# Output products of a four-layer hybrid trunk: plain products against Strassen's seven block products

## The chip, the cores and the metric

The kernel runs on one core of a Trainium2 chip. The metric is the device time of one execution in microseconds; the median of three runs stands for a kernel. The trace is that of one profiled execution. Five engines matter: TensorE (PE, matmuls and transposes), VectorE (DVE), ScalarE (ACT), GpSimd (POOL) and SyncE (SP), whose queue starts the DMAs. Each engine runs its own queue strictly in order, and engines wait for each other on semaphores.

## The reference

A decoder trunk of four layers on x of 1024 tokens by 1024 features, float32. Each layer normalizes, mixes tokens and adds an output product:

```python
for layer in range(DEPTH):                  # 4
    xn = rms_norm(x, norm_w[layer])
    kind, idx = layer % N_MIXERS, layer // N_MIXERS   # fox, gla, gdn, fox
    ...
    x = x + y.astype(x.dtype)
# each mixer ends with
    return (o * jax.nn.silu(z)) @ w_out     # o, z: 1024 x 1024; w_out: 1024 x 1024
```

FoX is softmax attention over 8 heads with a forget gate, GLA a gated linear attention over 4 heads, GDN (Gated DeltaNet) a chunked delta rule over 8 value heads. The change concerns the last line, `(o silu(z)) @ w_out`, and the addition to x.

## The kernel before, in words

Every float32 product is made of rounded parts: a value is split into `hi` (rounded, on ACT, L118) and `lo` (the rest, a subtraction on DVE, L119; `Trunk.split`), and `Trunk.mm3` issues three matmuls, hi by hi (L123), hi by lo (L124) and lo by hi (L125). The array `act` holds the transposed left side of the product at hand in both parts, eight token tiles of 128 by eight K tiles of 128 features.

A layer runs in this order. `Normed.scale` and `Normed.turn` scale a token tile by its norm (L63) and transpose it on PE (L207, into PSUM banks `pt`); L118 and L119 split it into `act`. The mixer projects its heads from `act`, computes them, gates them, and puts o into `oT` (FoX, already transposed: L411 on POOL multiplies by the gate) or `oN`/`og`/`o` (GLA, GDN), from where it goes into `act` again. Then `Trunk.out_proj` (L212) walks over chunks of output columns, 384, 384 and 256 wide in FoX, four of 256 in GLA and GDN (`MixPool.OUT`). `wchunk` loads and splits the chunk's weights. For each token tile a PSUM bank `pj` collects 8 K tiles by 3 matmuls, DVE adds it to x in place (L225), and ACT takes the sum of squares of the new x (L230). With the last chunk each finished token tile is stored, its norm taken (`rsqrt`, L130 on POOL), scaled and transposed for the next layer, tile by tile while later tiles are still in the product.

In FoX, the attention of a query tile t runs logits (`pq`), row maximum on DVE (L362), exponential on ACT (L369, `Lg`), scaling on DVE (L373), transposes on PE (L383, L387), a split (`PT<-pt`, L118 and L119), and the product with V (`pv<-PT,V`), which ACT copies to `oT` (L398).

The order of each engine's queue is not written by hand: the kernel is built in a context that schedules by a simulated timeline, within the program's dependences and the buffers of `MixPool` (tags with a number of buffers each; a new tile waits for the release of the old one). Weight chunks of the output product have buffers of their own among the weights, so its first matmuls can be placed between the last ones of the mixer.

## Time and profile before

| | us |
|---|---|
| median of 3 runs | 2326.18 |
| lowest, highest | 2325.18, 2328.27 |
| span of the profiled execution | 2328.1 |
| PE busy | 2256.5 (97%) |
| DVE busy | 1284.5 (55%) |
| ACT busy | 1026.5 (44%) |
| POOL busy | 424.5 (18%) |

The profiled execution's own time is its span of 2328.1 us, from the first to the last instruction; it is close to the slowest of the three runs. Busy time is the sum of an engine's instructions; matmuls overlap each other in the pipe, so one lasts longer in a row than the distance to the next. The granted clock of PE is given as a share of full speed. The trace puts the output products (first to last L225) at 556.9 to 649.8, 1012.5 to 1106.6, 1595.3 to 1712.7 and 2235.6 to 2325.1 us.

### The profile page before, as it was taken

The page shows a single profiled execution, that of the slowest core. Times are in us where ns is not written, and L with a number is a line of the kernel's source. Part 1 is how long each engine was busy: PE and PEld are TensorE (multiplying, and loading weights), DVE is VectorE, ACT ScalarE, POOL GpSimd, SP SyncE. Part 2 cuts the span into 40 slices and gives each one's busy share as a digit, 9 for nine tenths or more (in the row PEclk, how much of TensorE's full clock was granted, in tenths as well). Part 3 has the DMA queues.
Part 4 walks back from the last instruction along what each step waited for, and adds up shares of the span by engine and source line. Part 5 has one row for each costly group of instructions (what it writes and reads, how often), then busy time and mean ns, then how long its engine had stood idle before and what let it go on. Part 6 is the DMA issues. An engine that isn't in the chain of part 4 may idle for free.

```text
span 2328.1 us, 41807 instructions
## 1 busy us (share of the span) xinstructions
PE 2256.5 (97%) x15694; PEld 2143.1 (92%) x15694; DVE 1284.5 (55%) x3564; ACT 1026.5 (44%) x3046; POOL 424.5 (18%) x680
## 2 busy tenths in 40 slices
...
DMA packets 177626, 140.93 MB, mean 61 GB/s; under 512 B 37232, under 2 KB 165104, under 8 KB 177424
## 3 DMA queue, kind: packets, MB, share of 16 engines
...
q8 instruction: 123, 2.02, 0.4%
q14 instruction: 79, 0.65, 0.1%
...
## 4 chain that ended last, share of the span: by engine, by line
PE 79%; DMA 8%; POOL 4%; DVE 3%; issue 2%; ACT 2%; SPq 1%; ACTq 0%; POOLq 0%; DVEq 0%
PE pj L123 20%; PE pj L125 20%; PE pj L124 19%; DMA raw<-in_fox_w_in_dram 4%; POOL xt L800 2%; POOL tm L798 2%; PE pv L124 2%; PE pv L125 2%; PE pt L207 1%; PE pt L387 1%; PE pv L123 1%; PE pq L123 1%; PE pq L125 1%; PE pq L124 1%; PE pt L383 1%
## 5 line engine op out<-in xcount | busy, mean ns | idle before, releaser
L123 PE MATMUL pj<-w,act 128*128 128x256 f32 (+3 forms) x2688 | 855.8, 319 | 20.5 <-DVE x L225 5.8
L125 PE MATMUL pj<-w,act 128*128 128x256 f32 (+3 forms) x2688 | 844.7, 314 | 0.0
L124 PE MATMUL pj<-w,act 128*128 128x256 f32 (+3 forms) x2688 | 843.3, 314 | 0.4 <-DVE w L163 0.2
L123 PEld LDWEIGHTS pj<-w,act 128*128 128x128 f32 x2688 | 512.9, 191 | 35.0 <-ACT w L162 8.5
L124 PEld LDWEIGHTS pj<-w,act 128*128 128x128 f32 x2688 | 513.1, 191 | 3.9 <-DVE w L163 1.4
L125 PEld LDWEIGHTS pj<-w,act 128*128 128x128 f32 x2688 | 511.8, 190 | 3.1 <-DVE act L119 0.6
L163 DVE SCALAR_TENSOR_TENSOR w<-raw,nw,w 128x256 fp32r<-128x256 f32 (+4 forms) x443 | 217.7, 511 | 164.0 <-ACT w L162 162.4
L162 ACT ACTIVATE w<-raw,nw 128x256 fp32r<-128x256 f32 (+4 forms) x443 | 212.1, 506 | 216.4 <-DMA raw<-in_fox_w_in_dram 146.9
L123 PE MATMUL pj<-act,w 128*128 128x256 f32 (+1 forms) x896 | 305.0, 340 | 1.4 <-ACT y L686 1.4
L125 PE MATMUL pj<-act,w 128*128 128x256 f32 (+1 forms) x896 | 303.6, 339 | 2.4 <-DVE w L163 2.2
L124 PE MATMUL pj<-act,w 128*128 128x256 f32 (+1 forms) x896 | 303.3, 339 | 0.0
L130 POOL TENSOR_TENSOR rs<-ss,mhalf 128x2 f32<-128x2 f32 (+2 forms) x152 | 112.0, 737 | 634.4 <-DVE ss L129 553.5
L125 PEld LDWEIGHTS pj<-act,w 128*128 128x128 f32 x896 | 172.9, 193 | 20.0 <-DVE w L163 3.5
L123 PEld LDWEIGHTS pj<-act,w 128*128 128x128 f32 x896 | 173.0, 193 | 17.7 <-ACT y L686 2.0
L124 PEld LDWEIGHTS pj<-act,w 128*128 128x128 f32 x896 | 172.8, 193 | 15.5
L225 DVE TENSOR_TENSOR x<-x,pj 128x256 f32<-128x256 f32 (+1 forms) x112 | 51.1, 457 | 156.4 <-PE pj L125 152.8
L369 ACT ACTIVATE Lg<-Lg,nm 128x128 f32<-128x128 f32 (+7 forms) x128 | 99.3, 776 | 60.4 <-DVE nm L368 53.6
L294 ACT ACTIVATE qk<-pj 128x128 f32<-128x128 f32 x256 | 68.5, 273 | 113.5 <-PE pj L125 80.9
L119 DVE TENSOR_TENSOR PT<-pt,PT 128x512 fp32r<-128x512 f32 (+1 forms) x160 | 97.5, 631 | 29.2 <-ACT PT L118 28.8
L118 ACT CAST PT<-pt 128x512 fp32r<-128x512 f32 (+1 forms) x160 | 80.8, 543 | 68.7 <-PE pt L387 68.7
L411 POOL TENSOR_TENSOR oT<-oT,g 128x256 f32<-128x256 f32 x64 | 46.4, 743 | 274.1 <-DVE g L408 234.8
L688 DVE SCALAR_TENSOR_TENSOR y<-u,cw,y 128x512 f32<-128x512 f32 x96 | 77.9, 814 | 26.4 <-ACT y L686 23.2
...
## 6 DMA issues: line engine op xcount, KB each, us to landing
raw<-in_fox_w_in_dram SPq DMA_DIRECT2D x123, 192.0 KB, 3.6
...
raw<-in_fox_w_in_dram SPq DMA_DIRECT2D x128, 64.0 KB, 2.1
...
```

The lines of the kernel that those rows point to most:

```text
L118: self.nc.scalar.copy(hi, src)
L119: self.nc.vector.tensor_tensor(lo, src, hi.bitcast(F32), ALU.subtract)
L123: mm(out, lhi, rhi, start=start, stop=False)
L124: mm(out, lhi, rlo, start=False, stop=False)
L125: mm(out, llo, rhi, start=False, stop=stop)
L130: self.nc.gpsimd.tensor_tensor(out, ss, self.mhalf[:, :n], ALU.pow)
L162: self.nc.scalar.activation(hi, r, AF.Copy, scale=f)
L163: self.nc.vector.scalar_tensor_tensor(lo, r, f, hi.bitcast(F32), ALU.mult, ALU.subtract)
L225: nc.vector.tensor_tensor(xr, xr, p, ALU.add)
L294: nc.scalar.activation(qk[:, i, :], p[:, i * DH:(i + 1) * DH], AF.Square, accum_out=ss[:, i:i + 1])
L369: nc.scalar.activation(L[:, :W], L[:, :W], AF.Exp, bias=nm[:, 0:1], accum_out=nm[:, 1:2])
L688: stt(y, u[:, j:j + 512], cw[:, j, blk:blk + 1], y, ALU.mult, ALU.add)
```

## The change

The output product A W (A = o silu(z)) is done on halves: A11, A12, A21, A22 are halves of tokens by halves of features, B11 to B22 halves of features by halves of output columns. Winograd's form of Strassen's scheme needs seven block products instead of eight, with S1 = A21 + A22, S2 = S1 - A11, S3 = A11 - A21, S4 = A12 - S2 on the left, and differences of the B blocks on the right (made in place in the raw buffers on POOL: L367, L369, L374, L380). Each product is 4 token tiles by 4 K tiles by 3 matmuls of 256 columns, and the whole is run twice (`i` = 0, 1), for 256 columns of each column half. Results are added to x on DVE straight from PSUM or on POOL from the intermediate U.

This is the loop that goes, in `out_proj`, and the end of `fox`:

```diff
-        for i, n in enumerate(mp.out_widths):
-            w = self.wchunk([(0, self.cols(w_out, c0, n=n))], n)
-            for t in range(NT):
-                xr = x[t][:, c0:c0 + n]
-                p = self.pj()[:, :n]
-                self.proj_tok(p, t, w, 0, n)
-                nc.vector.tensor_tensor(xr, xr, p, ALU.add)
-                if nxt is None:
-                    nc.sync.dma_start(dst[t][:, c0:c0 + n], xr)
-                    continue
-                sq = mp.tile([P, D], mybir.dt.bfloat16, tag=mp.roles["sq"], name="sq")
-                nc.scalar.activation(sq[:, :n], xr, AF.Square, accum_out=parts[:, t, i:i + 1])
-                if i + 1 == nch:
-                    nc.sync.dma_start(dst[t], x[t])
-                    ss = total[:, t:t + 1]
-                    nc.vector.tensor_reduce(ss, parts[:, t, :], mybir.AxisListType.X, ALU.add)
-                    nxt.scale(t, ss)
-                    nxt.turn(t - 2)
-            c0 += n
         gate(H - 2)
         gate(H - 1)
-        for t in range(NT):
-            self.split(self.act[:, t, 0], self.act[:, t, 1], oT[t // 2][:, :, t % 2 * P:t % 2 * P + P])
...
+        mp.to_tail()
+        return self.sides_sb(mp, oT)
```

And this is what comes: the left sides from SBUF (`sides_sb`, FoX), from transposes (`sides_ps`, GLA and GDN), then the new `out_proj`:

```diff
+    def sides_sb(self, mp, oT):
+        b = self.blocks(mp)
+        at = lambda n, j, part: b[n][:, 2 * j:2 * j + 2, part]
+        view = lambda j, h: oT[j][:, 4 * h:4 * h + 4, :].rearrange("p h (e c) -> p e h c", c=P)
+        gt, tt = self.nc.gpsimd.tensor_tensor, self.nc.vector.tensor_tensor
+        def made(eng, x, y, op):
+            out = mp.tile([P, 2, KT // 2, P], F32, tag="L", name="sf")
+            eng(out, x, y, op)
+            return out
+        for j in range(2):
+            self.split(at("A11", j, 0), at("A11", j, 1), view(j, 0))
+            self.split(at("A12", j, 0), at("A12", j, 1), view(j, 1))
+        for j in range(2):
+            s1 = made(gt, view(j + 2, 0), view(j + 2, 1), ALU.add)
+            s2 = made(tt, s1, view(j, 0), ALU.subtract)
+            self.split(at("S1", j, 0), at("S1", j, 1), s1)
+            s4 = made(tt, view(j, 1), s2, ALU.subtract)
+            self.split(at("S2", j, 0), at("S2", j, 1), s2)
+            self.split(at("S4", j, 0), at("S4", j, 1), s4)
+            s3 = made(gt, view(j, 0), view(j + 2, 0), ALU.subtract)
+            self.split(at("A22", j, 0), at("A22", j, 1), view(j + 2, 1))
+            self.split(at("S3", j, 0), at("S3", j, 1), s3, gt)
+        return b
...
+        part = lambda n, t, src, eng=None: self.split(b[n][:, t, 0], b[n][:, t, 1], src, eng)
+        tag, n = mp.roles["raw"]
+        keep = [mp.tile([P, n, 4, P], F32, tag=tag, name="af") for _ in range(NT // n)]
+        kept = lambda h, t: keep[(4 * h + t) // n][:, t % n]
+        for t in range(NT // 2):
+            for h, p in enumerate(banks(t)):
+                part(("A11", "A12")[h], t, p)
+                nc.scalar.copy(kept(h, t), p)
+        for t in range(NT // 2):
+            g = banks(NT // 2 + t)
+            p = next(g)
+            s1 = mp.tails.tile([P, 4, P], F32, tag="s1f", name="s1f", bufs=2)
+            s3 = mp.tails.tile([P, 4, P], F32, tag="s3f", name="s3f", bufs=1)
+            s2, s4 = kept(0, t), kept(1, t)
+            nc.scalar.copy(s1, p)
+            tt(s3, s2, p, ALU.subtract)
+            p = next(g)
+            tt(s1, s1, p, ALU.add)
+            part("A22", t, p)
+            part("S1", t, s1)
+            gt(s2, s1, s2, ALU.subtract)
+            part("S3", t, s3)
+            gt(s4, s4, s2, ALU.subtract)
+            part("S2", t, s2, gt)
+            part("S4", t, s4, gt)
...
+        def load(i, r, c):
+            raw = mp.tail_tile([P, KT // 2, N], f"raw{2 * r + c}")
+            c0 = c * (D // 2) + i * N
+            nc.sync.dma_start(raw, w_out[r * (D // 2):(r + 1) * (D // 2), c0:c0 + N]
+                              .rearrange("(k p) c -> p k c", p=P))
+            return raw
+        def parted(raw):
+            w = mp.tailw.tile([P, KT // 2, 2, N], F32R, tag="ws", name="ws", bufs=3)
+            self.split(w[:, :, 0], w[:, :, 1], raw)
+            return w
+        side = [0]
+        def times(n, w):
+            side[0] += 1
+            banks = [(self.pj if side[0] % 2 else self.pq)() for _ in range(2)]
+            for t in range(H):
+                out = banks[t // 2][:, t % 2 * N:t % 2 * N + N]
+                for k in range(KT // 2):
+                    self.mm3(out, b[n][:, t, 0, k], b[n][:, t, 1, k], w[:, k, 0], w[:, k, 1],
+                             t % 2 == 0 and k == 0, t % 2 == 1 and k == KT // 2 - 1)
+            return [p.rearrange("p (t c) -> p t c", c=N) for p in banks]
...
+        def add(i, half, col, vs, eng=None, final=False):
+            cs = slice(col * (D // 2) + i * N, col * (D // 2) + i * N + N)
+            eng = eng or tt
+            for u in range(2):
+                j = half * 2 + u
+                if xp[j] is not None:
+                    eng(xp[j][:, :, cs], xp[j][:, :, cs], vs[u], ALU.add)
+                else:
+                    for e in range(2):
+                        xr = x[2 * j + e][:, cs]
+                        eng(xr, xr, vs[u][:, e], ALU.add)
...
+        for i in range(nch):
+            last = nxt is not None and i + 1 == nch
+            B11, B21, B12, B22 = (load(i, r, c) for r, c in ((0, 0), (1, 0), (0, 1), (1, 1)))
+            U = mp.tail_tile([P, 2, 2, N], "U")
+            U = [U[:, u] for u in range(2)]
+            p = times("A11", parted(B11))
+            for u in range(2):
+                nc.scalar.copy(U[u], p[u])
+            add(i, 0, 0, p)
+            add(i, 0, 0, times("A12", parted(B21)), final=True)
+            gt(B11, B12, B11, ALU.subtract)
+            w = parted(B11)
+            gt(B11, B22, B11, ALU.subtract)
+            p = times("S1", w)
+            add(i, 1, 1, p)
+            add(i, 0, 1, p)
+            w = parted(B11)
+            gt(B21, B21, B11, ALU.subtract)
+            p = times("S2", w)
+            for u in range(2):
+                tt(U[u], U[u], p[u], ALU.add)
+            add(i, 0, 1, U, gt)
+            w = parted(B22)
+            gt(B12, B22, B12, ALU.subtract)
+            add(i, 0, 1, times("S4", w), final=True)
+            p = times("S3", parted(B12))
+            for u in range(2):
+                tt(U[u], U[u], p[u], ALU.add)
+            add(i, 1, 1, U, gt, True)
+            add(i, 1, 0, U, gt)
+            if last:
+                ready(0)
+            add(i, 1, 0, times("A22", parted(B21)), final=True)
+            if last:
+                ready(1)
```

`mp.to_tail()` closes the memory of the weights and of the mixer; S1, S2, S4, U, two pairs of x and the split weights `ws` (3 buffers) go there. FoX loads the raw blocks into old buffers: B11 and B12 into those of `PT`, B21 and B22 into those of `bias`. `ready(0)` and `ready(1)` (store, norm, scale, transposes) run for four token tiles at once, after the S3 product and after the last one. In GDN the load of `og` gets two buffers and `mul(t)` moves ahead of all transposes. `MixPool.BELOW`, `XTAIL` and `HOMES` place the tiles.

The queues move at three places. In the order rows, the number behind a name tells buffers apart, and line numbers are those of the kernel that the row comes from.

**End of FoX.** PE's queue before, around the last products with V (`pv<-PT,V`); the matmuls of 384 columns are those of the output product:

```order
L125 MATMUL pj<-w,act 128x384
L123 MATMUL pv<-PT,V 128x256
L123 MATMUL pj<-w,act 128x384
L124 MATMUL pj<-w,act 128x384
L125 MATMUL pj<-w,act 128x384
L123 MATMUL pj<-w,act 128x384
L124 MATMUL pv<-PT,V 128x256
L125 MATMUL pv<-PT,V 128x256
L123 MATMUL pv<-PT,V 128x256
```

PE's queue now, at the last products with V:

```order
L123 MATMUL pv<-PT,V 128x256
L124 MATMUL pv<-PT,V 128x256
L125 MATMUL pv<-PT,V 128x256
L123 MATMUL pv<-PT,V 128x128
L124 MATMUL pv<-PT,V 128x128
L125 MATMUL pv<-PT,V 128x128
L123 MATMUL pj<-ws,act 128x256 x2
L123 MATMUL pq<-ws,act 128x256 x2
L124 MATMUL pj<-ws,act 128x256
```

From the transposes of the last head's last logits to the end of its products with V, 67 matmuls of the output product stood among them before; now none does, and the first block product follows the last `pv`.

ACT's queue before, from the last exponential of the last head (L369) to the sums of squares:

```order
L369 ACTIVATE Lg,nm<-Lg,nm 128x1024
L118 CAST act<-oT 128x1024 x4
L398 ACTIVATE oT<-pv 128x256
L407 ACTIVATE g<-pj 128x512
L118 CAST PT<-pt 128x512 x2
L118 CAST act<-oT 128x1024 x2
L118 CAST PT<-pt 128x512
L118 CAST PT<-pt 128x384
L398 ACTIVATE oT<-pv 128x256
L118 CAST act<-oT 128x1024 x2
L230 ACTIVATE sq,xss<-x 128x384 x6
```

ACT's queue now, from the same exponential (L523):

```order
L523 ACTIVATE Lg,nm<-Lg,nm 128x1024
L118 CAST act<-oT 128x2x512
L118 CAST PT<-pt 128x512 x3
L118 CAST PT<-pt 128x384
L552 ACTIVATE oT<-pv 128x256
L118 CAST S_6559<-sf 128x2x512
L118 CAST S_6560<-sf 128x2x512
L118 CAST S_6561<-sf 128x2x512
L118 CAST ws<-raw_6630 128x4x256
L118 CAST ws<-raw_6632 128x4x256
L118 CAST act<-oT 128x2x512
L118 CAST act<-sf 128x2x512
```

Three splits of S blocks (`S<-sf`) stand ahead of the first split weights (`ws<-raw_6630`, B11), and both behind the last copy of `pv`. On DVE the low parts stand in the same order (three of S, then `ws`).

**End of GLA.** POOL's queue before, from the last gates (L1021) to the next layer:

```order
L1021 TENSOR_TENSOR g<-g,gain 128x256 x5
L130 TENSOR_TENSOR rso<-ssh,mhalf 128x8
L1021 TENSOR_TENSOR g<-g,gain 128x256 x6
L130 TENSOR_TENSOR rs<-xst,mhalf 128x1 x7
L652 MEMSET tri 128x128
L655 MEMSET all_12125 128x128
L680 MEMSET u 128x3
```

POOL's queue now, from the same gates (L1176):

```order
L1176 TENSOR_TENSOR g<-g,gain 128x256 x5
L130 TENSOR_TENSOR rso<-ssh,mhalf 128x8
L1176 TENSOR_TENSOR g<-g,gain 128x256 x6
L287 TENSOR_TENSOR af<-s1f,af 128x512
L289 TENSOR_TENSOR af<-af 128x512
L119 TENSOR_TENSOR S_10955<-af,S_10955 128x512
L367 TENSOR_TENSOR raw_11157<-raw_11161,raw_11157 128x1024
L119 TENSOR_TENSOR S_10956<-af,S_10956 128x512
L287 TENSOR_TENSOR af<-s1f,af 128x512
L380 TENSOR_TENSOR raw_11161<-raw_11163,raw_11161 128x1024
L289 TENSOR_TENSOR af<-af 128x512
L369 TENSOR_TENSOR raw_11157<-raw_11163,raw_11157 128x1024
```

S2 (L287), S4 (L289), their low parts (L119) and the differences of the weights (L367, L380, L369) now alternate on POOL ahead of the products that use them.

**Start of GLA**, after the first FoX layer. PE's queue before, where the last product ends (256 columns) and the transposes of the new x stand (L207):

```order
L124 MATMUL pj<-w,act 128x256
L125 MATMUL pj<-w,act 128x256
L207 MATMUL pt<-ident,xn 128x128 x12
L123 MATMUL pj<-w,act 128x272 x2
L207 MATMUL pt<-ident,xn 128x128 x4
L124 MATMUL pj<-w,act 128x272
L125 MATMUL pj<-w,act 128x272
L123 MATMUL pj<-w,act 128x272
L124 MATMUL pj<-w,act 128x272
```

PE's queue now, within the first projections of GLA:

```order
L123 MATMUL pj<-w,act 128x272
L124 MATMUL pj<-w,act 128x272
L125 MATMUL pj<-w,act 128x272
L207 MATMUL pt<-ident,xn 128x128 x40
L123 MATMUL pj<-w,act 128x272
L124 MATMUL pj<-w,act 128x272
```

The transposes came in pieces of 4 to 12 between matmuls; now 40 stand in one piece, behind the projections of two token tiles and ahead of the third.

## Rows read from the trace of the kernel before

**Rows 1.** Page, part 1: busy time, share of the span and instructions, by engine.

```profile
PE 2256.5 (97%) x15694; PEld 2143.1 (92%) x15694; DVE 1284.5 (55%) x3564; ACT 1026.5 (44%) x3046; POOL 424.5 (18%) x680
```

**Rows 2.** Page, part 4: shares of the chain that ended last, by engine.

```profile
PE 79%; DMA 8%; POOL 4%; DVE 3%; issue 2%; ACT 2%; SPq 1%; ACTq 0%; POOLq 0%; DVEq 0%
```

**Rows 3.** Windows in two output products: stretch, length, busy us (xcount) of PE, PEld, DVE, ACT, POOL; clock, DMA.

```profile
580.00:600.00 20.00, 20.00 (x116) 20.00 (x115) 6.61 (x13) 6.35 (x18) 0.00 (x0) 1.00 0.20 60
1030.00:1050.00 20.00, 20.00 (x172) 20.00 (x171) 5.73 (x12) 5.85 (x18) 0.00 (x0) 1.00 0.30 103
```

**Rows 4.** Windows at the ends of output products and the starts after them.

```profile
540.00:650.00 110.00, 110.00 (x712) 108.15 (x712) 47.90 (x95) 37.17 (x89) 7.89 (x13) 1.00 0.25 88
650.00:660.00 10.00, 8.82 (x67) 7.74 (x64) 8.71 (x19) 7.33 (x17) 0.55 (x1) 1.00 0.52 140
660.00:670.00 10.00, 7.71 (x46) 7.26 (x46) 4.41 (x13) 4.61 (x11) 0.00 (x0) 0.83 0.52 122
1110.00:1120.00 10.00, 7.58 (x56) 6.79 (x55) 5.98 (x12) 4.19 (x9) 1.43 (x3) 0.94 0.01 0
1610.00:1620.00 10.00, 8.37 (x67) 7.43 (x66) 6.07 (x14) 5.36 (x16) 0.70 (x1) 1.00 0.46 143
1620.00:1630.00 10.00, 8.82 (x75) 8.61 (x73) 2.23 (x5) 1.76 (x4) 0.00 (x0) 1.00 0.48 160
1630.00:1640.00 10.00, 6.88 (x36) 6.38 (x36) 3.89 (x8) 4.28 (x11) 0.00 (x0) 0.66 0.41 117
1640.00:1650.00 10.00, 6.26 (x40) 6.26 (x41) 4.98 (x11) 4.99 (x12) 0.00 (x0) 0.83 0.53 151
1650.00:1660.00 10.00, 9.50 (x78) 9.09 (x77) 3.88 (x10) 4.56 (x14) 0.00 (x0) 1.00 0.50 108
2190.00:2310.00 120.00, 120.00 (x711) 114.81 (x710) 55.96 (x145) 37.60 (x87) 7.17 (x10) 1.00 0.30 93
```

**Rows 5.** Waits of PE in 1590 to 1670 us: us in total, times, longest.

```profile
PE pj L123 <- DVE x L225: 5.4, 4, 4.2
PE pj L123 <- ACT w L118: 3.7, 1, 3.7
```

**Rows 6.** Timeline of all engines, 547 to 550 us: start, us, operation, xcount.

```profile
547.74 1.16 ACT L369 ACTIVATE Lg<-Lg,nm 128x1024 f32<-128x1024 f32 x1 [1.46 <-DVE nm L368]
549.21 0.75 DVE L373 TENSOR_SCALAR Lg<-Lg,ri 128x1024 f32<-128x1024 f32 x1
```

**Rows 7.** Groups by line and form on ACT, DVE and POOL: xcount | busy us, mean ns.

```profile
L118 ACT CAST act<-oT 128x1024 fp32r<-128x1024 f32 x16 | 15.7, 1043 | 4.8 <-POOL oT L411 4.8
L118 ACT CAST act<-pt 128x512 fp32r<-128x512 f32 x96 | 55.4, 585 | 32.9 <-PE pt L207 32.7
L119 DVE TENSOR_TENSOR act<-oT,act 128x1024 fp32r<-128x1024 f32 x16 | 18.7, 1221 | 1.7 <-ACT act L118 1.7
L119 DVE TENSOR_TENSOR act<-pt,act 128x512 fp32r<-128x512 f32 x96 | 65.6, 688 | 22.4 <-ACT act L118 21.7
L163 DVE SCALAR_TENSOR_TENSOR w<-raw,nw,w 128x256 fp32r<-128x256 f32 x176 | 86.3, 525 | 50.0 <-ACT w L162 49.1 <-DMA U<-xs 0.3
L63 DVE TENSOR_SCALAR xn<-x,rs 128x1024 f32<-128x1024 f32 x32 | 24.4, 761 | 10.8 <-POOL rs L130 10.8
L225 DVE TENSOR_TENSOR x<-x,pj 128x256 f32<-128x256 f32 x80 | 33.4, 419 | 79.7 <-PE pj L125 76.1 <-DMA x<-xs 3.2
L762 POOL TENSOR_TENSOR Dc<-Dc,gc 128x1024 f32<-128x1024 f32 x8 | 18.2, 2276 | 22.9 <-DMA Dc<-gcd 12.1 <-PE pj L125 10.8
```

**Rows 8.** Timeline of all engines, 1172.5 to 1178 us.

```profile
1172.75 2.08 POOL L762 TENSOR_TENSOR Dc<-Dc,gc 128x1024 f32<-128x1024 f32 x1 [0.23 <-DMA Dc<-gcd]
1172.98 4.98 DVE L163 SCALAR_TENSOR_TENSOR w<-raw,nw,w 128x256 fp32r<-128x256 f32 x4
1174.78 0.38 POOL L682 COPY u<-u 128x3 f32<-128x3 f32 x1
1175.12 2.57 POOL L763 TENSOR_SCALAR_AFFINE_SELECT Dc<-Dc 128x1024 f32<-128x1024 f32 x2
```

116 lines of the change are left out of this document (89 added, 27 removed).

## The prediction

> **What bounds the kernel now.** I read the profile from the whole to the place. Part 1 of the page comes first: PE is busy for 97% of the span, DVE for 55%, ACT for 44%, POOL for 18% [rows 1]. The chain that ended last is PE for 79% [rows 2]. So time falls only where PE has fewer columns to stream, and it rises wherever PE's queue comes to stand. POOL looks idle, but a share of a span says nothing about one place, so I read the places next. Inside an output product PE is full at a clock of 1.00: 116 matmuls of 384 columns in 20 us (0.172 us each) and 172 of 256 columns (0.116 us each) [rows 3]. The ends and starts show two kinds of place [rows 4]. The ends of the FoX layers are full (540 to 650 and 2190 to 2310 us), since the output product is mixed into the end of attention. The starts of GLA and GDN and the end of GDN have holes, and behind holes the granted clock falls: at 1630 to 1640 us it is 0.66, so a part of that stretch ran at the lower of the two levels (1.2 instead of 2.4 GHz).
>
> **The change, part by part.** The sum stands against the profiled execution's 2328.1 us, which is 1.9 above the median of 2326.18. About 0.2% (4.7 us) is what a measurement of this kernel can tell from no change.
>
> (a) *Matmuls removed.* FoX had 2 x 192 matmuls of 384 and 192 of 256 columns, 384 x 0.172 + 192 x 0.116 = 88.3 us; GLA and GDN 768 x 0.116 = 89.1 us. Now each layer has 7 x 48 x 2 = 672 of 256 columns, 78.0 us [rows 3] (as many matmuls in the whole as before, but narrower ones in FoX). That is 10.3 us for each FoX layer and 11.1 for the others: **-42.8 us**, the only certain gain, since PE bounds these stretches.
>
> (b) *Ends of the two FoX layers.* The order shows 67 matmuls of the output product among the last head's transposes and PV products; at 0.172 us they gave PE 11.5 us of other work [rows 3]. Now nothing is placed there, as the products need whole blocks and memory that attention holds. The dependent steps below them stay: the last row's exponential and scaling (1.16 and 0.75 us [rows 6]), one `act` split of 1.04 and four PT splits of about 0.585 on ACT, the last low part 0.69 on DVE [rows 7], some 6.0 us before the last PV can run, partly beside PE's own transposes. Between 0 and 11.5 I take 7. Behind the last PV, ACT copies `pv` (a PT split's 0.585 at most), splits three S blocks (3 x 1.04), then B11 (1.04), and DVE makes B11's low part (1.22): 6.0 us [rows 7]; I take 7, since the S blocks wait for POOL's `sf`, at 2.28 us a piece by the row of the same size on POOL. So each FoX layer gains a hole of 14 us. The clock will fall behind it: the window at 0.83 loses 1.7 us of ten, the one at 0.66 3.4 [rows 4]; I take 2.5. Two layers: **+33** (bounds: +12, no hole before the last PV and no fall of the clock, to +42, with 11.5, 6.0 and 3.4).
>
> (c) *End of GLA.* A11 needs its transposes split on ACT and also copied for S (8 x 0.585 = 4.7 us for four banks [rows 7]) before `ws`. With the clock **+6** (0 to 9).
>
> (d) *End of GDN.* Between 1610 and 1660 us PE was busy for 39.8 of 50 us, and its clock lost another 5.1 [rows 4]; two waits make up most of it, for the addition to x and for split weights [rows 5], because the next layer's weights stand ahead of this product's in SP's queue. In the new order all blocks of the first half are loaded early, so these 15.3 us go. In their place come the last chain steps with only 13 matmuls between them (3), the splits ahead of A11 (4.5, as in c), S1 and S2 (3) and the clock (2.5): **-2** (-15 to +8).
>
> (e) *Starts of the next layers.* `ready(1)` hands over four token tiles when the last product ends. DVE then needs 4 x (0.76 + 2 x 0.69) + 4 x 0.42 = 10.2 us [rows 7], with the norm's steps on DVE and POOL about 12.5. PE has 48 matmuls of 272 columns beside it (48 x 0.116 x 272/256 = 5.9) and then 40 transposes in one piece, so it stands for some 6.5 us, 8.2 with the clock. Before, GLA's start cost 1.2 + 2.3 + 1.7 = 5.2 us (650 to 670), GDN's 2.4 + 0.6 = 3.0 [rows 4]. Three starts, the last taken like GDN's: **+13** (0 to 16). The kernel's end has a final addition of 512 instead of 256 columns: **+0.3**.
>
> (f) *POOL beside DVE.* The change puts on POOL what DVE did not do before: per layer four differences of weights of 128x1024 (2.28 us each [rows 7]) and S parts. The trace shows what happens to DVE then: four L163 from 1172.98 us took 4.98 us where their mean gives 4 x 0.525 = 2.1 [rows 7, 8], while POOL worked for 5.0 us [rows 8]. So 2.9 us are lost in 5.0 of POOL's. At a FoX end three `sf` and a low part, 4 x 2.28 = 9.1 us, stand beside DVE's S and weight parts, which read SBUF twice as L163 does: 9.1 x 0.58 = 5.3 us, twice 10.6. In GLA and GDN POOL has 16 operations of 512 (half of 2.28) and four of 1024, 27 us, for S2 and S4 that are due 16.8 and 22.4 us after A11 starts (three and four products of 48 x 0.116); I take 4 each. **+19** (0 to +32; a gain is excluded, as no DVE operation is shortened by POOL's work).
>
> The Trainium skill, "SBUF — State Buffer", section "SBUF: two separate sides", states that DVE and GpSimd share a port pair as an exclusive lock, and that a DVE operation with two SBUF inputs and a GpSimd operation that reads SBUF block each other for the whole instruction. The trace agrees that they hurt each other, though 4.98 us are less than the 7.1 that full exclusion of 2.1 and 5.0 would give. Taken whole, the rule would put the sum at the rival of full exclusion below.
>
> Sum: -42.8 + 33 + 6 - 2 + 13 + 0.3 + 19 = +26.5. Against the profiled span 2354.6, by the median **2353 us**, slower by 1.1%.
>
> **The rivals.**
> *No contention.* If DVE's and POOL's operations don't meet on the path (f = 0), the sum is +7.5: 2334 us. For it: DVE operations that read PSUM, such as L225, are no case of L163, and the in-place differences wait for DVE's low part first, so some can't overlap.
> *Full exclusion.* DVE waits for each of POOL's operations to end. Then the FoX ends lose POOL's whole 9.1 us instead of 5.3, twice, and GLA and GDN 3 more each, since their S parts alternate with DVE's: 2 x 3.8 + 2 x 3 = 13.6 us more than the forecast, 2367 us. (It is the rule of the Trainium skill's page cited above.) For it: the longest stretch that the trace shows is only 5 us [rows 8], and here POOL works in a row for 20.
> *Faster: the holes are short.* One mechanism: the S blocks and B11 are ready when the last PV ends, so the FoX hole is the unfilled tail alone. It decides at the point where ACT is done with S and B11's high part at the last PV's end: then the FoX ends cost 2 x 7, with the clock 2 x 8.5 = 17; POOL is done early too (f = 0), and the starts are as before (e = 0). With -42.8 + 17 + 6 - 9 (a middle of d's bounds and its gain) + 0.3 = -28.5 the time is 2328.1 - 28.5 - 1.9 = 2298 us. For it: POOL is 82% idle, and 43 us are a certain gain. Against it: in ACT's queue these splits stand behind the last copy of `pv`.
> *The change doesn't save columns.* If products from S tiles ran slower than 0.116 us, as where PSUM banks in alternation bind, (a) would shrink; nothing in the rows speaks for it, and at half the saving the time is 2353 + 21 = 2374 us.
>
> **How the numbers follow.** Forecast 0.42 (2340 to 2362), no contention 0.2 (2326 to 2342), full exclusion 0.12, faster 0.23 (2285 to 2318), no saving 0.03. No change takes about half of the second case: 0.10. Faster by over 0.2% (below 2321.5) gets 0.23 and a share of the second case's lower bounds: 0.25. Slower is the rest, 0.65. The range runs from 2294, just under the centre of the faster case, to 2378; it leaves out some 0.1 of that case, and 0.06 of full exclusion and no saving.
>
> **What would show it.** Right: the output products keep 2 x 576 + 2 x 768 = 4 x 672 = 2688 matmuls, but all of 256 columns, at 0.116 us where PE doesn't wait; PE's windows behind both FoX ends hold a hole of 12 to 22 us, ended by ACT or DVE on `ws` or S; DVE's low parts of S and `ws` have means well above 1.22 us; the windows of GDN's end are full again; the starts have 6 to 8 us of hole before 40 transposes. Wrong: the FoX holes under 8 us, or DVE's low parts at 1.22 us beside POOL's work. The forecast falls to the faster case if PE's idle time, clock included, grows by less than 43 us in the four transitions together.

## The result, and the profile after

| | before | after |
|---|---|---|
| median of 4 runs, us | 2325.68 | 2410.43 |
| lowest, highest | 2323.48, 2328.27 | 2408.17, 2414.23 |
| span of the profiled execution | 2328.1 | 2406.5 |
| mean granted clock | 0.984 | 0.961 |

The changed kernel is slower: ratio 1.0365, interval 1.0349 to 1.038. The forecast was 2353 us in 2294 to 2378. The sign was right, the size (27 us) a third of what came (85 us in the medians, 78.4 between the two profiled spans).

The page of after, parts 1 and 4 (against [rows 1, 2]):

```profile
PE 2261.6 (94%) x15694; PEld 2128.6 (88%) x15694; DVE 1443.5 (60%) x3612; ACT 1091.1 (45%) x3114; POOL 665.7 (28%) x808
...
PE 72%; DMA 7%; DVE 7%; POOL 6%; issue 4%; ACT 3%; SPq 1%; ACTq 0%; DVEq 0%; POOLq 0%
```

PE's busy time hardly changed (2256.5 to 2261.6), although its products have 42.8 us fewer columns to stream. So the saving was eaten inside the busy time, for the most part by a slower clock, and idle time came on top. The shares of DVE and POOL on the chain that ended last grew (to 7 and 6%).

PE's queue holds the same work in both kernels but for four stretches, each from the end of a mixer into the next layer. The windows of these stretches, first before, then after (stretch, length, then busy time and count of PE, PEld, DVE, ACT, POOL, then granted clock, DMA share, GB/s):

```profile
459.40:664.30 204.90, 201.22 (x1265) 191.95 (x1263) 111.32 (x303) 86.20 (x238) 20.85 (x31) 1.00 0.26 75
1000.20:1114.00 113.80, 113.44 (x962) 113.23 (x961) 50.79 (x107) 40.01 (x110) 8.17 (x16) 1.00 0.31 109
1542.50:1810.90 268.40, 256.39 (x1904) 249.63 (x1903) 141.38 (x395) 117.66 (x374) 32.65 (x45) 0.98 0.27 83
2138.80:2328.10 189.30, 186.29 (x1154) 178.65 (x1152) 88.61 (x249) 60.05 (x163) 15.34 (x21) 1.00 0.24 72
```

```profile
461.10:693.60 232.50, 205.93 (x1362) 192.89 (x1360) 156.54 (x312) 103.97 (x261) 77.50 (x57) 0.91 0.24 73
1029.90:1155.40 125.50, 112.42 (x867) 107.94 (x865) 93.22 (x127) 61.20 (x143) 74.48 (x52) 0.92 0.36 120
1582.60:1870.10 287.50, 257.46 (x1807) 243.28 (x1807) 175.96 (x420) 136.29 (x400) 97.24 (x85) 0.94 0.26 79
2198.10:2406.50 208.40, 186.44 (x1249) 177.15 (x1247) 127.97 (x251) 72.80 (x163) 69.33 (x47) 0.93 0.21 68
```

From these rows: change of length; PE idle time (length less PE busy); the columns saved, term (a); and what is left, which is PE busy on the same work for longer. "Forecast" puts the prediction's terms on the stretches.

| stretch | length | idle | columns | left: busy longer | forecast length |
|---|---|---|---|---|---|
| first FoX end, GLA start | +27.6 | +22.9 | -10.3 | +15.0 | +14.5 |
| GLA end, GDN start | +11.7 | +12.7 | -11.1 | +10.1 | +4.1 |
| GDN end, last FoX start | +19.1 | +18.0 | -11.1 | +12.2 | -3.9 |
| last FoX end | +19.1 | +19.0 | -10.3 | +10.4 | +11.8 |
| sum | +77.5 | +72.6 | -42.8 | +47.7 | +26.5 |

The column "busy longer" is not all clock. The trace records the granted clock over time; laid over PE's busy time in the four stretches, the lower level cost 14.4, 7.3, 10.9 and 9.6 us after, against 0, 0, 4.1 and 0 before. That is 38.2 us more. The other 9.5 of the 47.7 us passed at full clock. Each break in the stream makes the busy time somewhat longer by itself: in e8 below, 48 matmuls at full clock take 6.02 us, where 48 x 0.116 is 5.6. At 0.4 us a break, 25 more breaks make some 10 us, which is an estimate.

The prediction's terms held some 63 us of new idle time and some 6 us of clock. The idle time came some 10 us larger than that; the clock's loss came six times as large.

**The first FoX end.** Windows of ten us of after:

```profile
550.00:560.00 10.00, 5.32 (x24) 3.80 (x23) 8.09 (x15) 4.33 (x7) 3.07 (x2) 0.74 0.32 105
560.00:570.00 10.00, 6.10 (x30) 5.76 (x30) 5.95 (x7) 4.53 (x7) 1.53 (x2) 0.67 0.37 129
570.00:580.00 10.00, 4.71 (x18) 4.12 (x19) 10.00 (x4) 4.60 (x5) 10.00 (x4) 0.50 1.02 394
580.00:590.00 10.00, 10.00 (x78) 10.00 (x77) 10.00 (x6) 4.63 (x6) 6.57 (x3) 0.89 0.01 3
590.00:600.00 10.00, 3.98 (x19) 3.61 (x19) 8.59 (x7) 2.22 (x9) 8.76 (x4) 0.79 0.00 1
...
610.00:620.00 10.00, 10.00 (x86) 10.00 (x85) 5.55 (x6) 4.04 (x10) 2.51 (x3) 1.00 0.30 96
```

PE stands for 19.9 us of these first five windows (5 x 10 less 30.1), where [rows 4] had them full, and the clock is at 0.50, the lower level, for all of 570 to 580. Once fed, PE does 86 matmuls of 256 columns in 10 us, 0.116 us each, so term (a) is as forecast. The waits of PE in this end and the GLA start (line waited for: total, times, longest):

```profile
PE pj L124 <- DVE ws L119: 9.9, 2, 5.5
PE pt L207 <- DVE act L119: 4.8, 6, 2.7
PE pt L541 <- DVE Lg L527: 4.4, 1, 4.4
PE pj L123 <- ACT ws L118: 4.2, 1, 4.2
```

The last PV row's chain (Lg), the first split of B11 on ACT, and twice DVE's low parts of weights: the kinds of hole that the forecast had, with about its sum (14 + 5.3 us an end) though not its sizes: 4.4 us ahead of the last PV, where it took 7, then 4.2 and 4.4 behind it, and 5.5 ahead of the product of S1. Why the low parts are late, DVE's timeline and then POOL's show (start, length, operation, count):

```profile
567.88 5.67 DVE L119 TENSOR_TENSOR S<-sf,S 128x1024 fp32r<-128x1024 f32 x3 [1.09 <-ACT S L118]
573.48 6.66 DVE L119 TENSOR_TENSOR ws<-raw,ws 128x1024 fp32r<-128x1024 f32 x2
580.07 3.40 DVE L119 TENSOR_TENSOR act<-oT,act 128x1024 fp32r<-128x1024 f32 x1
```

```profile
569.19 6.56 POOL L236 TENSOR_TENSOR sf<-oT 128x1024 f32<-128x1024 f32 x2 [1.47 <-DVE S L119]
575.72 3.35 POOL L119 TENSOR_TENSOR act<-sf,act 128x1024 fp32r<-128x1024 f32 x1
579.02 3.36 POOL L367 TENSOR_TENSOR raw<-raw,raw 128x1024 f32<-128x1024 f32 x1
```

Both engines show the same 3.3 us for one operation, where [rows 7] had 1.22 us for DVE's and about 2.28 for POOL's: they work in turns. Over the whole kernel, the groups by line (busy, mean ns):

```profile
L119 DVE TENSOR_TENSOR ws<-raw,ws 128x1024 fp32r<-128x1024 f32 x56 | 100.3, 1796 | 31.8 <-ACT ws L118 31.8
...
L336 DVE TENSOR_TENSOR x<-x,pj 128x512 f32<-128x512 f32 x40 | 26.7, 680 | 20.3 <-PE pj L125 15.4 <-POOL x L336 4.9
...
L119 DVE TENSOR_TENSOR S<-sf,S 128x1024 fp32r<-128x1024 f32 x12 | 24.8, 2090 | 1.3 <-ACT S L118 1.3
```

**The GDN end and the last FoX start.** The waits of PE there, the largest two:

```profile
PE pt L264 <- DMA og<-ogd: 7.1, 1, 7.1
PE pj L123 <- ACT w L162: 6.0, 3, 2.3
```

The old stall of 15.3 us is gone from its place, the product of GDN, but the sign that the prediction set, full windows at GDN's end, did not come: PE has 16.7 us of idle time from 1582.6 to 1740 us and 13.4 in the start behind it. Two waits stand there that no term held: a load of `og` back from memory, and the split weights of the last FoX layer, which arrive late. SP's queue from 1630 to 1800 us shows what stood ahead of the second:

```profile
SPq L351 <- DVE x L340: 33.7, 1, 33.7
```

The store of a finished token tile heads the queue for 33.7 us, and the next layer's weights, loaded from 1613 to 1657 us before, are loaded from 1737 to 1782 us.

### The profile page after: what moved, and what is told of

It reads as the page before. It is cut to its first block, busy times and chain, and to the rows that moved or that the text cites. A ratio compares the mean times of both kernels' runs of the same rounds, so it can differ in the third digit from the quotient of the medians.

```text
span 2406.5 us, 42048 instructions
## 1 busy us (share of the span) xinstructions
PE 2261.6 (94%) x15694; PEld 2128.6 (88%) x15694; DVE 1443.5 (60%) x3612; ACT 1091.1 (45%) x3114; POOL 665.7 (28%) x808
## 4 chain that ended last, share of the span: by engine, by line
PE 72%; DMA 7%; DVE 7%; POOL 6%; issue 4%; ACT 3%; SPq 1%; ACTq 0%; DVEq 0%; POOLq 0%
PE pj L123 16%; PE pj L125 16%; PE pj L124 16%; DMA raw<-in_fox_w_in_dram 4%; PE pq L123 3%; PE pq L124 3%; PE pq L125 3%; POOL xt L954 2%; POOL tm L952 2%; PE pv L124 1%; PE pv L125 1%; PE pt L541 1%; PE pv L123 1%; DVE w L163 1%; PE pt L537 1%
## 5 line engine op out<-in xcount | busy, mean ns | idle before, releaser
L123 PE MATMUL pj<-w,act 128*128 128x384 f32 (+3 forms) x1792 | 586.3, 328 | 19.7 <-ACT w L162 12.6
L124 PE MATMUL pj<-w,act 128*128 128x384 f32 (+3 forms) x1792 | 575.0, 321 | 0.5 <-DVE w L163 0.4
L125 PE MATMUL pj<-w,act 128*128 128x384 f32 (+3 forms) x1792 | 574.9, 321 | 0.4 <-DVE act L119 0.4
L123 PEld LDWEIGHTS pj<-w,act 128*128 128x128 f32 x1792 | 342.3, 191 | 34.0 <-ACT w L162 17.1
L124 PEld LDWEIGHTS pj<-w,act 128*128 128x128 f32 x1792 | 343.1, 192 | 4.5 <-DVE w L163 2.1
L125 PEld LDWEIGHTS pj<-w,act 128*128 128x128 f32 x1792 | 341.8, 191 | 3.5 <-DVE act L119 1.1
L163 DVE SCALAR_TENSOR_TENSOR w<-raw,nw,w 128x256 fp32r<-128x256 f32 (+4 forms) x443 | 223.9, 526 | 161.0 <-ACT w L162 158.8
L162 ACT ACTIVATE w<-raw,nw 128x256 fp32r<-128x256 f32 (+4 forms) x443 | 212.1, 506 | 232.8 <-DMA raw<-in_fox_w_in_dram 149.5
L523 ACT ACTIVATE Lg<-Lg,nm 128x128 f32<-128x128 f32 (+7 forms) x128 | 99.4, 777 | 72.0 <-DVE nm L522 64.0
L119 DVE TENSOR_TENSOR ws<-raw,ws 128x1024 fp32r<-128x1024 f32 x56 | 100.3, 1796 | 31.8 <-ACT ws L118 31.8
L119 DVE TENSOR_TENSOR PT<-pt,PT 128x512 fp32r<-128x512 f32 (+1 forms) x160 | 97.8, 632 | 30.1 <-ACT PT L118 29.7
L1176 POOL TENSOR_TENSOR g<-g,gain 128x256 f32<-128x256 f32 x64 | 46.9, 734 | 247.6 <-DVE g L1174 241.4
```

The costliest lines, as they stand in the source:

```text
L119: (sub or self.nc.vector.tensor_tensor)(lo, src, hi.bitcast(F32), ALU.subtract)
L123: mm(out, lhi, rhi, start=start, stop=False)
L124: mm(out, lhi, rlo, start=False, stop=False)
L125: mm(out, llo, rhi, start=False, stop=stop)
L162: self.nc.scalar.activation(hi, r, AF.Copy, scale=f)
L163: self.nc.vector.scalar_tensor_tensor(lo, r, f, hi.bitcast(F32), ALU.mult, ALU.subtract)
```

## The experiments

The theory after the result was: holes are made by DVE's and POOL's turns and by chains ahead of the first product, and each hole costs clock beyond its length. Rivals: the turns alone; places in memory and the order of the queues alone.

### e1: DVE and POOL by themselves

A small kernel with operations of the sizes used here: DVE alone, both together, and DVE with other kinds of operands.

```diff
+    for _ in range(6):
+        tt(dc, da, db, ALU.subtract)
+        gt(pc, pa, pb, ALU.subtract)
...
+        tt(dc[:, :256], da[:, :256], banks[1][:, :256], ALU.add)
...
+        nc.vector.tensor_scalar(dc, da, 0.5, None, ALU.mult)
```

> Computes nothing of the reference: it runs additions and subtractions of 128x1024 float32 in SBUF on DVE and POOL, first each engine alone, then both at once, then DVE with one operand in PSUM, then DVE with a single SBUF input, each beside POOL; afterwards PE streams matmuls of 256 columns with holes of about 2, 4, 7 and 13 us and then eight short holes between pieces of 48 matmuls. Theory 1 (the two engines exclude each other): alone DVE takes 1.22 us and POOL about 2.1; together each pair takes their sum, 3.3 us, and both rows read 3.3 or alternate; with the operand in PSUM DVE keeps its 0.42 us. Rival (a stretched DVE has another cause in the trunk, the DMAs or ACT): together they keep 1.22 and 2.1 us within 20%. On the clock: if holes set it, the granted clock stays at the upper level after the short single holes and falls behind the longer ones or the repeated ones; if it is no matter of holes, all streams run at 0.116 us a matmul.

The timeline of DVE, then of POOL:

```profile
21.90 16.77 DVE L68 TENSOR_TENSOR dc<-da,db 128x1024 f32<-128x1024 f32 x5
...
41.04 1.22 DVE L68 TENSOR_TENSOR dc<-da,db 128x1024 f32<-128x1024 f32 x1
42.29 2.24 DVE L58 TENSOR_TENSOR dz<-dc,dy 128x1 f32<-128x1 f32 x1
44.64 2.70 DVE L72 TENSOR_TENSOR dc<-da,b 128x256 f32<-128x256 f32 x6
```

```profile
25.18 15.76 POOL L69 TENSOR_TENSOR pc<-pa,pb 128x1024 f32<-128x1024 f32 x5
```

Beside each other, DVE's five took 16.77 us (3.35 each, in a row) and POOL's 15.76 (3.15); alone, the DVE one took 1.22. While POOL worked, DVE's additions with one operand in PSUM kept their 0.42 us (0.409 to 0.422). So the two exclude each other nearly whole, where the prediction took 0.58 of POOL's time: with POOL's 2.34 to 2.41 us beside those additions, taking turns to the full would be 3.6 us. The part of this kernel that was to price holes of PE failed: ACT's copies ran ahead, and the holes were not of the length meant. Its eight holes of 0.82 us, with 48 matmuls between them, cost nothing beyond themselves (6.02 us for each 48). e8 does that part again.

### e2: nothing of the change on POOL

```diff
-        tt, gt = nc.vector.tensor_tensor, nc.gpsimd.tensor_tensor
+        tt = gt = nc.vector.tensor_tensor
```

> Only change against the changed kernel: all additions and subtractions that it put on POOL (S parts, low parts, differences of weights, x += U) run on DVE. Theory 1 (the turns of DVE and POOL make the holes): low parts of ws fall from 1.80 to 1.22 us, a pair costs 2.4 instead of 3.3 us, the holes at the FoX ends shrink by 6 to 10 us each and the clock with them; the time falls by 20 to 45 us, to 2365 to 2390. Rival (the order of the queues makes the holes whichever engine works, or DVE becomes the bound): the time stays within 10 us of 2410 or rises.

2386.87 us, ratio 1.0263 (1.0236 to 1.0289), 23.6 us under the changed kernel and in what was expected. The stretches became 224.4, 120.3, 287.0 and 200.0 us: 8.1, 5.2, 0.5 and 8.4 shorter, though DVE does all the work. Net of the work that DVE takes over, POOL's part cost about this much, near term (f)'s 19; but 61 us of the loss stay.

### e3: dummy matmuls in the holes of the FoX ends

```diff
+        def idle(n, count):
+            d = self.psum("pr")
+            for k in range(count):
+                self.nc.tensor.matmul(d[:, :N], b[n][:, 0, 0, 0], b[n][:, 0, 0, 1:3],
+                                      start=k == 0, stop=k == count - 1)
...
+                idle("A11", 50)
+                idle("S1", 50)
```

> Adds to the changed kernel, in the FoX layers only, 140 matmuls a layer whose result nobody reads (16.3 us of PE at 0.116 us): 50 that need A11 alone, 50 that need the first S1 block, 40 between the products A12 and S1. They stand in PE's queue where it has nothing else. Theory 2 (the granted clock that falls behind the holes costs as much as the holes): in spite of 16.3 us more work per layer the first FoX end gets shorter by 3 to 10 us, its clock loss falls from 21.6 us to under 12, and the time falls by 5 to 20 us. Rival (the clock is a small term, holes are all): the added matmuls fill holes at no gain or lengthen the path; the time stays or rises by up to 20 us.

2416.19 us, ratio 1.0393 (1.0376 to 1.0411): 6 more, not less. About 5 us of them lie where no dummy is: the span before the first stretch grew by that much, with 2602 matmuls against 2601; why is not known. In the first stretch itself 139 more matmuls (16.1 us by 0.116) left the length at 232.7 us; idle time fell by 10.8, the clock rose from 0.91 to 0.95. So the clock gave back about 5 us (16.1 - 10.8 - 0.2), as much as the dummies cost beyond the holes. The loss by the clock that is left (232.7 x 0.05, some 12 us) is what was expected of it, the time is not. Filler without use wins nothing here, and the price of the clock stayed open.

### e4 and e12: the change in some kinds of layer alone

```diff
+STRASSEN = {'gdn', 'gla'}
...
+        self.plain = kind not in STRASSEN
...
+                if mp.plain:
+                    self.out_proj_plain(a[kind + "_w_out"][idx], x, dst, mp, xT)
```

> Strassen's products in GLA and GDN only; the two FoX layers keep the plain output product of the kernel before, with its memory. By the trace of the changed kernel the stretches around the ends of GLA and GDN lost 12 and 19 us, those of the two FoX ends 28 and 19. If the losses belong to the layer whose product is changed, the time is about 2326 + 31 = 2357 us, within 10; if they come from the memory or from the loads that the change moves everywhere, it stays near 2410 or falls to 2330.

> Strassen's products in the two FoX layers only; GLA and GDN keep the plain product. With the run for GLA and GDN alone at 2368 us (42 more than before), the two kinds should add up to the change's 84 if they don't touch each other: 2368 here, within 8. If the start of the layer behind (plain memory, loads that come early) carries part of the loss, less.

GLA and GDN alone (e4): 2367.94 us, ratio 1.0181 (1.0166 to 1.0196), just above its range. FoX alone (e12, with `{'fox'}`): 2391.25 us, 1.0271 (1.0254 to 1.0288). The losses, 1.81 and 2.71%, add up to more than the change's 3.65%, and e12 lies above its range. Its waits at the last FoX layer's start tell why:

```profile
PE pj L123 <- ACT w L162: 13.7, 6, 3.9
```

The first weights come at 1725.7 us, where PE already waits for them; here even with a plain product in GDN. That the memory is laid out for the FoX end to come is the likely reason; it was not tried by itself. A layer's end can't be priced alone: where memory lies decides when the next layer can load.

### e5 and e6: `og` earlier; the first product of A before the S blocks

```diff
-            o = mp.tails.tile([P, D - 2 * P], F32, tag="og", name="og", bufs=2)
+            o = (mp.tile([P, D - 2 * P], F32, tag="kq", name="og") if t < NT // 2
+                 else mp.tails.tile([P, D - 2 * P], F32, tag="og", name="og", bufs=2))
```

> Changed kernel, but in GLA and GDN the transposes and splits of token tiles 0 to 3 (A11, A12) are traced ahead of the turn of the memory, and GDN's load of og for these tiles goes into four old buffers of the mixer (tag kq) instead of two in memory that lies over the mixer's. Theory (in GDN PE waits 7.1 us for og, because its place is only free when the mixer ends, and that wait was not in the forecast): the stretch around GDN's end falls by 7 to 14 us with the clock, GLA's and FoX's stay within 2 us; time about 2396 to 2404. Rival (S parts on POOL would be late anyway): the wait moves behind og, the time stays within 4 us of 2410.

2405.35 us, 1.0339 (1.032 to 1.0357), between its two ranges; the interval overlaps the changed kernel's. The wait for `og` fell from 7.1 to 3.4 us, but the stretch only from 287.5 to 285.5: waits for `w`, `act`, `ws` and `af` of 2.0 to 3.9 us each took its place. A single wait taken away gives little where several chains end close together.

e6 has that and also the first two products from buffers of their own, ahead of the memory that the S blocks need:

```diff
+        self.early(mp, b)
+        mp.to_tail()
+        self.blocks_s(mp, b)
...
+            p = self.first[0] if given else times("A11", parted(B11))
```

> As the run before, and the first two block products (A11 B11 and A12 B21 of the first half) take weights that are loaded and split into the mixer's own weight buffers, as in the kernel before, and stand ahead of the turn of the memory in all layers: 96 matmuls of 256 columns that PE can run between the last products of the mixer. B11 and B21 are loaded a second time for the differences. Theory (the FoX ends lost their filler, and splits of S and B11 stand in a row behind the last PV): the hole before the last PV goes, the one behind it shrinks since S1 is all that is waited for; each FoX end gains 12 to 25 us, clock included, GLA and GDN some 5 each; time 2350 to 2385. Rival (the turns of POOL and DVE for S and T set the end whatever PE has before): PE runs out of work at S1 instead, and the time falls by under 15 us.

2403.24 us, 1.0333 (1.0315 to 1.0351); the rival with under 15 us was right. The scheduler does mix these products into the end of attention, and the windows are full up to 568 us. The hole then comes in one piece:

```profile
570.00:580.00 10.00, 0.00 (x0) 0.00 (x0) 10.00 (x7) 6.20 (x9) 8.88 (x3) 0.54 1.04 396
580.00:590.00 10.00, 0.80 (x2) 0.50 (x2) 10.00 (x6) 4.54 (x10) 8.84 (x4) 0.50 0.26 103
```

```profile
PE pj L123 <- ACT ws L118: 19.6, 1, 19.6
```

So the lost filler isn't the bound of the FoX ends: what stands ahead of the product of S1 takes that long, whatever PE does in the meantime. DVE is busy for all 20 us, but not all of the hole is DVE's and POOL's work. S1's weights are B12 less B11, and the last piece of them finds its place only when the last PV ends. SP's queue issues its load at 570.36 us, behind four loads of `x` (the second row is its time from issue to landing, in us):

```profile
570.36 0.38 SPq L331 DMA_DIRECT2D raw<-in_fox_w_out_dram  x1
DMA to landing us min/median/max: 8.5/8.5/8.5
```

The hole begins at 568.4 us, so until 578.8, for 10.4 us, it follows from that load, and with the difference and the split behind it for some 14 (an estimate). The row of DVE and POOL adds the rest. In the changed kernel itself that piece landed at 575.4 us, ahead of POOL's difference (L367, 579.02), so there DVE and POOL did set the hole. No run moved this load.

### e7 and e10: both together

> The run before with all additions of the change on DVE instead of POOL. If turns of DVE and POOL and lost filler are separate causes, the gains add: 2410 less 23 (measured for no POOL alone) less what the run before gains, 2330 to 2360. If they are the same hole, the time is that of the run before, within 8 us.

2378.05 us, 1.0228 (1.0202 to 1.0254), above what was expected and not near its rival. The gains of e2 (23.6 us) and e6 (7.2) simply add up: 2410.43 less both is 2379.6. So they have separate causes. Without POOL's turns the hole is still there, with DVE's own work in a row:

```profile
PE pj L123 <- DVE sf L238: 15.8, 1, 15.8
```

```profile
580.00:590.00 10.00, 0.80 (x2) 0.50 (x2) 10.00 (x12) 6.12 (x12) 0.00 (x0) 0.50 0.36 143
```

Ten us of DVE hold 12 operations now, where 6 stood. Here too the last piece of weights is loaded late, at 571.00 us and with 8.6 us to landing, so 10.4 of the hole's 15.8 us follow from it. e10 has in addition the stores of e9:

> The best of the earlier runs together: first two products early with weights of their own, no additions on POOL, and the stores of x on ACT's queue. If the store's wait is a cause of its own, the time is that of the run with the first two (2378) less the gain of the store alone, 2358 to 2372; if it is none, 2374 to 2382. A time under 2326 would need the S chain of some 20 us behind each mixer to be hidden, and nothing hides it: not expected.

2373.15 us, 1.0195 (1.018 to 1.021). That lies between its two ranges and settles nothing on the stores (e9 does). It is the best form of the whole change that ran, and still 2% slower than plain products.

### e8: the price of PE's holes

A small kernel: streams of matmuls of 256 columns, with holes made by a chain of dependent copies on ACT.

```diff
+    for k in (1, 2, 4, 8):
+        piece(k, 400)
+    for k in (1, 2, 4):
+        for _ in range(6):
+            piece(k, 48)
+        piece(1, 400)
```

> Computes nothing of the reference: PE streams 400 matmuls of 256 columns (46.5 us at 0.116), with single holes of about 2.5, 3.5, 5.5 and 9.5 us between such streams, then three groups of six holes (2.5, 3.5, 5.5 us) with 48 matmuls (5.6 us) between them. Theory (the clock falls behind holes, and repeated ones cost more than their own length): the streams behind the longer holes begin at 0.23 us a matmul, and pieces of 48 behind repeated holes of 3.5 us and more run at half clock, 11 us each. Rival (the clock is set by something else of the trunk): all pieces of 48 take 5.6 to 6.1 us.

PE's timeline (length of the stream, its count, and in brackets the hole ahead of it):

```profile
111.31 48.26 PE L49 MATMUL b<-R,L 128*128 128x256 f32 x400 [3.14 <-DVE R L61]
164.80 49.63 PE L49 MATMUL b<-R,L 128*128 128x256 f32 x400 [5.24 <-DVE R L61]
223.97 50.62 PE L49 MATMUL b<-R,L 128*128 128x256 f32 x400 [9.54 <-DVE R L61]
276.60 7.50 PE L49 MATMUL b<-R,L 128*128 128x256 f32 x48 [2.01 <-DVE R L61]
...
295.73 6.02 PE L49 MATMUL b<-R,L 128*128 128x256 f32 x48 [2.07 <-DVE R L61]
...
568.75 8.38 PE L49 MATMUL b<-R,L 128*128 128x256 f32 x48 [5.24 <-DVE R L61]
```

A single hole of 2.0 or 3.1 us in a long stream costs nothing beyond itself; one of 5.2 costs 1.4 us more, one of 9.5 2.4 us (against 48.26). But with 48 matmuls between holes, as many as one block product has, even holes of 2 us cost 1.5 us more in four of six cases (7.50 against the 6.02 that the two others show), holes of 3.1 us 1.3 to 2.6, and holes of 5.2 us 1.5 to 2.4 us. The 11 us that were expected for 48 matmuls behind a long hole did not come (7.4 to 8.6), nor did the rival's 6.1 throughout.

### e9: stores in another queue

```diff
-                nc.sync.dma_start(dst[t], x[t])
+                nc.scalar.dma_start(dst[t], x[t])
```

> Only change against the changed kernel: the stores of the new x, which stand in front of the next layer's weights in SP's queue and wait there 34 to 41 us for the last additions, are issued from ACT's queue instead. Theory (a wait that the forecast did not see: next layer's first weights come late because SP stands at the store): these weights are loaded while the last products still run, the holes of the three starts shrink, by most at the last FoX layer, where the start costs some 20 us with the clock; time falls by 8 to 20 us. Rival (the weights could not come earlier anyway, since their place lies over the S blocks, or the starts are bound by the transposes of four tiles at once): within 4 us of 2410.

2411.25 us, 1.0351 (1.033 to 1.0373): no gain. SP's queue now waits with the weight load itself:

```profile
SPq L152 <- PE pj L125: 32.3, 1, 32.3
```

The rival was right: the store only stood in front; the weights have no place before the product's last matmuls let go of theirs.

### e11: the kernel before, without the filler of the FoX ends

```diff
+                with (self.tc.issue_after(self.hold) if mp.W.get('wz') and i == 0 else nullcontext()):
+                    self.proj_tok(p, t, w, 0, n)
```

> The kernel before, with one ordering edge: in the FoX layers the matmuls of the first chunk of the output product stand behind the last product with V in PE's queue; no work is added or left out. It measures what the lost filler alone costs. The forecast took 7 us of hole and 2.5 us of clock for each FoX end: 2345 us. If the clock's price is that of every single hole (1.5 to 2.4 us for each of three to four holes), each end costs 10 to 14 us: 2346 to 2354. Rival (the filler was only moved, the end is bound elsewhere): 2326 to 2332.

2337.54 us, 1.0042 (1.0029 to 1.0055): +10, between its two ranges. The two FoX stretches became 210.4 and 195.1 us, 5.5 and 5.8 longer. So of a FoX end's loss the missing filler makes 5 or 6 us, clock included. In the first of them PE's idle time grew by 3.9 us, in three holes of at most 1.4, and its busy time by only 1.6: short holes cost less, so there is no fixed price for one.

### e13 to e17: the kernel before, with the last FoX layer's weights held back

Here the loads of these weights (L152) are put behind a load or a store of GDN's output product.

```diff
+            if i == 1:
+                self.behind = self.load.ins
...
+            with self.tc.issue_after(self.behind) if h == 0 and xT.src is None else nullcontext():
+                w = self.wchunk(loads, 3 * DH + f, rows=xT.nw, raws=raws)
```

> The kernel before, with one ordering edge on SP's queue: the loads of the last FoX layer's first weights (44 loads, 1613 to 1657 us before) stand behind the loads of GDN's second chunk of the output product instead of between them. No work changes. Theory (in the kernel before these early loads cost the stall in GDN's product and pay for a start of the last FoX layer without holes; the change turns that round): the stall of 15 us at 1610 to 1660 goes or shrinks, and the start stays nearly full since the loads end before it; 2312 to 2322. Rival (the stall comes from the splits or the additions, not from the loads): 2324 to 2330.

> The same with the edge behind the third chunk's loads (about 1665 us): the loads then end near the start of the last FoX layer (about 1710 us). Theory: GDN's stall gone, the start begins to wait for its weights; 2312 to 2326.

> The same with the edge behind the last chunk's loads (about 1690 us), the nearest that the plain kernel comes to the changed one, whose loads ran from 1736 to 1782 us, at the start itself. Theory (late weights are what the last FoX layer's start lost with the change): the start opens holes of 10 to 25 us with the clock, the stall of 15 us is gone, 2320 to 2338. Rival (the start of the changed kernel is bound by the 40 transposes and the four tiles handed over at once): the start stays full here too, 2310 to 2316.

2325.94 (ratio 0.9999, 0.999 to 1.0009), 2330.26 (1.0013, 1.0003 to 1.0022) and 2328.54 us (1.001, 0.9997 to 1.0022): no gain, and e14, whose interval leaves out 1, is some 3 us slower. But GDN's stall moves with these loads. Before, they are issued from 1614 to 1653 us, and PE stands for 10.2 of the 50 us from 1610 to 1660 [rows 4]. In e15 they are issued from 1650 to 1684 us, and these waits stand there from 1645 to 1690 us:

```profile
DVE w L163 <- ACT w L162: 23.7, 10, 5.8
ACT w L162 <- DMA raw<-in_fox_w_in_dram: 22.1, 10, 4.5
PE pj L123 <- DVE x L227: 10.5, 3, 5.2
```

ACT's and DVE's splits of the next layer's weights (L162, L163) stand in these engines' queues ahead of the product's additions to `x` (L227), and wait there for their loads; PE then waits for the additions. So term (d) was right that the next layer's weights make the stall, if through ACT's and DVE's queues, and wrong that it would go: it stands where the loads stand. The next two go further, behind the store of token tile 3 (e16) and of tile 7 (e17):

> The kernel before, with one ordering edge on SP's queue: the loads of the last FoX layer's first weights for q, k and v (11 of 192 KB and their small pieces) stand behind GDN's store of token tile 3 (about 1700 us) instead of at 1613 to 1657. The three runs before let them begin at 1650 at the latest and the start stayed full. Theory (late weights are what the last FoX layer's start lost with the change): with loads from 1700 to some 1745 us the start at 1712 waits, with holes of 5 to 15 us and clock; 2330 to 2345. Rival (the start is bound by the hand-over of four tiles and the transposes in one piece, which this kernel doesn't have): the start stays full, within 4 us of 2326.

> The same behind the last store (about 1712 us), which is where the changed kernel has them: from the start of the layer itself. Theory: holes of 12 us and a clock loss of 8 us as in the changed kernel's start (1740 to 1800 us there), or more; 2340 to 2360. Rival: within 4 us of the run behind store 3.

e16 took 2324.06 us (0.9993, 0.9983 to 1.0003), e17 2335.42 us (1.0045, 1.003 to 1.006), below its range. In e17 these loads are issued from 1693 to 1727 us, all behind the product. The rows show the product and the 60 us behind it, first before, then e17, and ten us of e17's start:

```profile
1595.30:1712.70 117.40, 107.23 (x863) 105.07 (x862) 52.76 (x120) 45.66 (x131) 5.96 (x10) 0.96 0.35 112
1712.70:1772.70 60.00, 58.16 (x347) 56.69 (x346) 32.07 (x112) 26.59 (x100) 9.34 (x13) 1.00 0.16 45
```

```profile
1588.80:1692.50 103.70, 102.39 (x864) 101.34 (x863) 46.94 (x109) 39.60 (x120) 5.94 (x10) 1.00 0.29 101
1692.50:1752.50 60.00, 46.35 (x211) 40.78 (x210) 22.89 (x64) 18.54 (x61) 4.73 (x7) 0.77 0.23 56
1720.00:1730.00 10.00, 6.56 (x19) 5.02 (x19) 5.00 (x16) 4.63 (x16) 1.40 (x2) 0.50 0.60 109
```

With the loads behind it the product is full: 13.7 us shorter for the same work, with 1.3 us of idle time where it had 10.2. The start pays for that and more: PE stands for 13.7 us of its first 60, where it stood for 1.8, and the clock is 0.77 instead of 1.00, down to 0.50, as in the changed kernel's start. So the 10 us that e17 lost (2335.42 against 2325.97 in the same comparison) are the net of a gain in the product and a larger loss at the start. In e16 (loads from 1678 us) the two balance: its product is full until 1680 us, and of the 40 us behind PE stands for 9.9. Its time came out as the rival had it, but not because the loads cost nothing.

## Why the prediction was wrong in size, step by step

(a) **Matmuls removed, -42.8.** Held: 86 matmuls of 256 columns in 10 us, 0.116 us each, where PE is fed.

(b), (f) **FoX ends and POOL beside DVE.** Their idle time held: 14 + 5.3 = 19.3 us forecast for an end, 19.9 measured in the first and 17.8 in the last. Its parts came near too: the unfilled tail has 4.4 us of idle time where 7 was taken, and costs 5 to 6 us with its clock (e11). The rest stands ahead of the B11 and S products. It is DVE's and POOL's work in the changed kernel; in e6 and e7, with holes of 19.6 and 15.8 us, some 10 us of each follow from a late load of weights. For f, the factor of 0.58 was wrong and the rival of full exclusion right in its mechanism: 3.3 us for either engine's operation (e1). The Trainium skill, "SBUF — State Buffer", section "SBUF: two separate sides", says so of a DVE operation with two SBUF inputs beside a GpSimd operation that reads SBUF (the one that starts first has the port pair for its whole instruction); e1's trace nearly agrees, 3.35 us being DVE's 1.22 and 2.1, nearly the 2.28 of POOL's operation in [rows 7]. Its worth in time is e2's 23.6 us against the 19 forecast (32.6 by that rival).

(c), (e) **GLA's end and the starts.** The stretch of GLA's end with GDN's start has 12.7 us more idle time; the forecast's terms for it, without clock, were 4.5 for the end, 4 for POOL and 4.1 for the start (6.5 less the 2.4 of before), 12.6. Right for the idle time; the clock's 7 us there, against 2.6 in these terms, belong to the step below.

(d) **GDN's end, -2.** Wrong by about 10 us of idle time, of which some 7 lie in the start behind it (13.4 us, where 6.5 was taken). The step took the stall of 15.3 us as gone and put nothing in its place at the next start. The stall left the product, but loads that go behind the product hold up the start instead (e17). Two waits came that the step never named: the reload of `og` (7.1 us), and weights of the next layer (6.0 us) that have no place before the product's last matmuls (e9). The step counted DVE's and ACT's work and left out what reuse of the mixer's memory does to the loads behind it.

**The step that failed most** is the clock: "I take 2.5" for an end, one fall for each. It came to some 38 us at the lower level instead of about 6, and to 47.7 with the breaks themselves. The trace of after has 28 waits of PE of 1 us or more in the four stretches (7, 7, 9 and 5, together 74 us), that of before 3 (all in the third stretch, 8.9 us). So 25 more holes share the 38 us, 1.5 us each, the lower end of what e8 measured for holes with one block's 48 matmuls between them: mostly 1.5 to 2.4 us each beyond their own length. The forecast summed nearly the right idle time but paid for its clock once per end and start. The division among the holes in the kernel itself is worked out, not measured; e3, which was to measure it there, gave back 5 us of clock in one stretch but nothing in the total.

With the count of holes from after, which the forecast didn't have, e8's prices give 25 x 1.5 to 25 x 2.4, so 37.5 to 60 us, in place of 6. With 10 us more for (d) the sum would have been 68 to 90.5; between the two profiled spans it is 78.4. That it lies inside doesn't show a price per hole, since the count is the measured one and the price varies (e11).
